# New prices in the planner that orders a two-block layer kernel

## The chip, the cores and the metric

The kernel runs on one core of a Trainium2 chip. The metric is the device time of one execution in microseconds; lower is better. The time before is the median of three executions, 1999.38 us (1998.83 to 1999.78).

## The reference

A sequence of 256 tokens with 1024 features passes through two stacks of two layers, all in float32.

The first stack has two hybrid layers. Each normalises its input, multiplies it by `w_in`, runs a short causal convolution, a gated delta rule in chunks of 64 over four heads, and a second gated convolution; it projects back with `w_out` and adds a gated feed-forward block of width 2816:

```python
def hybrid_layer(x, ...):
    h = rms_norm(x, norm1_g)
    proj = h @ w_in
    ...
    o_dn = chunk_gated_delta_rule(q, k, v, g, beta)
    ...
    x = x + jnp.concatenate([o_dn, o_sc], axis=-1) @ w_out
    h2 = rms_norm(x, norm2_g)
    x = x + (jax.nn.silu(h2 @ ffn_w_gate) * (h2 @ ffn_w_up)) @ ffn_w_down
    return x
```

The second stack has two layers of three sub-blocks each: a feed-forward block, a token mixer, a feed-forward block. Each sub-block's input is normalised and shifted by a modulation vector (`silu(c) @ mod_w`, nine vectors of 1024 per layer), and its output is normalised, scaled and added. The token mixer has a diagonal state-space branch (32 groups of 64 states, a recurrence along the tokens) and an attention branch with a forgetting gate (8 heads), whose results are gated, merged and projected.

## The kernel before, in words

**The products.** Activations lie transposed, features on the 128 partitions and 256 tokens along the row. Every weight matrix is streamed once, in blocks of 128x1024 words (512 KB): eight tiles of 128x128. The products are of type `float32r`; to keep the accuracy, weights and activations are split into a high and a low part, and each tile takes three products (`group`, L258 to L274). `prepare` (L219 to L245) brings one block: a load into `wr` (four buffers) on SP's queue at L228, the high part `wh` by ScalarE (L234; a few by VectorE, L232), the low part `wl` by VectorE (L241; four buffers). `wblk` keeps four blocks (`AHEAD`) prepared ahead of the one in use. A group's sums lie in four PSUM banks with the tag "g", which VectorE or ScalarE must read before the next group may start.

**Work beside the products.** The modulation vectors are 144 steps on VectorE, each with a load of 512 KB into a single buffer `mraw` (`mod_step`, L494 to L502, paced by `MOD_RATE`). `ssm_params` (L1104 to L1192) prepares a layer's state-space tables: it runs inside the feed-forward block ahead of the mixer, as a long chain of 128x512 products on VectorE (L1116, the helper `tt`), then transposes (L1159, copied out by ScalarE at L1160) and small products of 32 columns (L1170). `ssm_tile` (L1194 to L1240) makes the recurrence: products (L1205), VectorE scans (L1218), and small products of 32 columns (L1230, L1237). The delta rule inverts its triangular matrices by rows (L827) and levels (L841 to L856). `narrow` (L295 to L319) makes eight-column projections with 32-column products (L311) on an operand made by VectorE at L303. In `ffn` (L414 to L458) VectorE multiplies the gate and the up group (L445) and with ScalarE splits the result (L372, L373).

**What sets the order.** The program is first written down in its natural order. Then `Order` (L1604 to L1899) takes the list of instructions, makes a graph of them with a price in nanoseconds for each (`price`, L1676 to L1703; loads at L1732 to L1741), latencies between engines (`LAT`) and the releases of buffers, and simulates a list schedule on all engines (`run`). `fix` does so forward and backward in turns, for four settings (`HOW`) of ten rounds each, the priorities of each round coming from the times of the round before, and keeps the plan with the shortest simulated span. The order of the starts in that plan becomes the order of the instructions on each engine. Nothing else of the plan is kept: each engine works through its list in that order, and each instruction still waits for what it needs. A load is two nodes: the issue on its queue, and the transfer at 360 bytes per ns in order of issue, `end`, some latency after the issue; a consumer starts 907 to 1000 ns after the transfer's end (last row of `LAT`):

```python
    LAT = [[0, 196, 197, 224, 240, 0, 0],
           ...
           [907, 1000, 985, 907, 907, 0, 0]]
```

VectorE's price at L1699 is (n + 66)/0.96 ns for an instruction with two full operands of n elements per partition: 1135 ns for n = 1024, 602 ns for n = 512.

Of the kernel before, what the change touches and what calls it, by code (L numbers as in the profile page):

```python
# [1603 lines left out]
class Order:  # L1604
# [71 lines left out]
    def price(s, e, x):  # L1676
        free = lambda y: int(np.prod([n for _, n in list(y.ap)[1:]]))
        real = lambda l: [y for y in l if getattr(y, "bass_ap", None) is not None]
        ins, outs = real(x.ins), real(x.outs)
        psum = any("PSUM" in str(y.bass_ap.space) for y in ins)  # L1680
        n = free(outs[0])
        if e == s.PE:
            n = free(ins[0])
            m = free(ins[1])
            if str(ins[0].dtype).endswith("float32r"):
                return max(n / 2.4, 92 if n > 64 else 80) + 2
            if m <= 32:
                return 150 if n > 64 else 60
            return (1 if getattr(x, "is_transpose", False) else 2) * (max(n / 1.2, 92) + 2)
        n = max(free(y) for y in ins + outs)  # L1690
        ptr = any(free(y) == 1 for y in ins)
        op = str(x.opcode)
        if e == s.DVE:
            if op == "Reciprocal":
                return (6 * n + 66) / 0.96
            if op == "Memset":
                return n / 0.96 + 8
            full = sum(free(y) > 1 or n == 1 for y in ins) > 1 or psum or op == "TensorReduce"
            return ((n if full else n / 2) + 66) / 0.96 + (61 if ptr and op == "TensorScalarPtr" else 0)  # L1699
        if e == s.ACT:  # L1700
            return n / 1.2 + (51 if psum else 94) + (93 if ptr and op == "Activation" else 0)
        same = any(list(y.ap)[-1][0] == 0 for y in ins)
        return 148 + n * (1.667 if same else 2.104)  # L1703


    def trace(s, instructions):
        live, room, rel, slots, alloc, queue = {}, {}, {}, {}, {}, {}
        opened, closed, shut, tags = set(), [], {}, {}
        acc = []
        for x in instructions:  # L1710
            if str(x.opcode) == "TilePoolBoundary":
                acc.append(None)
            else:
                acc.append(s.accesses(x) if len(x.outs) else [])
        last = {}
        for i, a in enumerate(acc):
            for r in a or ():
                last[r[0].name] = i
        for x, a in zip(instructions, acc):
            if a is None:  # L1720
                n = x.bass_pool_name
                if n in opened:
                    opened.discard(n)
                    closed.append(n)
                else:
                    opened.add(n)
                    shut[n] = (s.node(s.NONE, 0), list(closed))
                continue
            if not len(x.outs):
                continue  # L1730
            e = s.NAMES[str(x.engine).split(".")[-1]]
            if str(x.opcode) == "DMACopy":  # L1732
                both = all(getattr(y, "bass_ap", None) is not None and hasattr(y.bass_ap.tensor, "tag_meta") for y in list(x.ins) + list(x.outs))
                i = s.node(e, {s.SP: 650 if both else 475, s.ACT: 100, s.POOL: 1038}[e], x)
                size = max(4 * int(np.prod([n for _, n in y.ap])) for y in list(x.ins) + list(x.outs))
                end = s.node(s.DMA, size / 360.0)
                s.edge(i, end, 650 if e == s.SP else 1100)
                if e in queue:
                    s.edge(queue[e][0], i, 0)
                    s.edge(queue[e][1], end, 0)  # L1740
                queue[e] = i, end  # L1741
            else:
                f = str(getattr(x, "func", "")).split(".")[-1]
                i = end = s.node(e, s.price(e, x), x, s.SETS.get(f) if e == s.ACT else None, s.shares(e, x))
            for r in a:
                t = r[0]
                if t.name in live:
                    continue
                tag = t.tag
                live[t.name] = []  # L1750
                rel[t.name] = s.node(s.NONE, 0)
                if tag in alloc:
                    s.edge(alloc[tag], i, -s.cost[alloc[tag]])
                alloc[tag] = i
                pool = next(n for n in sorted(shut, key=len, reverse=True) if tag.rsplit("_", 1)[0].endswith("_" + n))
                tags.setdefault(pool, []).append(t.name)
                sl = slots.setdefault(tag, [])
                if len(sl) == t.tag_meta.bufs:
                    o = min(sl, key=last.get)
                    sl.remove(o)  # L1760
                    room[t.name] = rel[o]
                else:
                    room[t.name] = shut[pool][0]
                sl.append(t.name)
            for t, w, p0, p1, f0, f1, ps in a:
                hits, keep = 0, []
                for q in live[t.name]:
                    qi, qe, qw, a0, a1, b0, b1 = q
                    hit = a0 < p1 and p0 < a1 and b0 < f1 and f0 < b1
                    hits += hit  # L1770
                    if hit and (w or qw) or ps:
                        near = e == qe and not (hit and qw)
                        s.edge(qi, i, 0 if near else s.LAT[qe][e])
                    if not (ps or w and p0 <= a0 and a1 <= p1 and f0 <= b0 and b1 <= f1):
                        keep.append(q)
                live[t.name] = keep
                if not hits:
                    s.edge(room[t.name], i, s.FREE2[e])
            for t, w, p0, p1, f0, f1, ps in a:
                live[t.name].append((end, s.eng[end], w, p0, p1, f0, f1))  # L1780
                s.edge(end, rel[t.name], s.FREE1[s.eng[end]])
        for n, (i, before) in shut.items():
            for o in before:
                for t in tags.get(o, ()):
                    s.edge(rel[t], i, 0)
# [137 lines left out]
```

## Time and profile before

| | |
|---|---|
| Median of three executions | 1999.38 us |
| The profiled execution's own time | 2000.42 us |
| Its span, first to last instruction | 1998.3 us |
| TensorE (PE) busy | 1888.2 us, 94% |
| VectorE (DVE) busy | 1516.6 us, 76% |
| ScalarE (ACT) busy | 1075.8 us, 54% |
| Read from memory | 380.12 MB, 191 GB/s |
| Chain that ended last, by engine | PE 84%, DVE 8%, ACT 3%, DMA 3%, issue 2% |
| Mean granted TensorE clock | 0.970 |

The share of an engine is its busy time over the span. The chain that ended last is followed back from the last instruction; each piece is an instruction or a transfer that the next piece waited for.

### The profile page before, as it was taken

The numbers are of one execution on the slowest core, as the hardware profiler recorded it, in microseconds if no ns is written. First come the engines' busy times: TensorE is split into PE (matmuls) and PEld (weight loads), VectorE is DVE, ScalarE is ACT, GpSimd is POOL, SyncE is SP. The second block draws the span as 40 slices with busy tenths as digits, with TensorE's granted clock in tenths as the row PEclk, the third lists the DMA queues.
The fourth block names the chain that finished last, engine by engine and source line by source line (L and its number), as shares of the span: only waits on it lengthen the run. The fifth ranks groups of instructions, "written<-read, shape, count | busy, mean of one in ns | idle before, by whom it ended". The sixth has DMA issues, their size and how long they took to land.

```text
span 1998.3 us, 40034 instructions
## 1 busy us (share of the span) xinstructions
PE 1888.2 (94%) x16106; PEld 1830.1 (92%) x16106; DVE 1516.6 (76%) x2826; ACT 1075.8 (54%) x1976; POOL 8.4 (0%) x20
## 2 busy tenths in 40 slices
PE   6999999899899986999999986999999999999998
PEld 6999999899899986999889986998999889999997
DVE  7888977898877788976784798867876677477554
ACT  6766544675544464445555653445554556565443
POOL 0000000000000000000000000000000000000000
PEclk8999999899999998999899998999999999999999
DMA  5334778433577763775343644775687443344553
GB/s 191 126 116 154 281 274 294 158 138 113 201 275 274 278 213 132 264 267 201 100 150 128 214 160 142 263 260 190 221 292 261 166 138 128 138 169 148 180 190 116
DMA packets 110921, 384.82 MB, mean 193 GB/s; under 512 B 16400, under 2 KB 16912, under 8 KB 110736
## 3 DMA queue, kind: packets, MB, share of 16 engines
q1 hardware_dynamic: 110448, 381.88, 54.5%
q8 instruction: 126, 2.06, 0.4%
q14 instruction: 59, 0.48, 0.1%
q10 hardware_dynamic: 288, 0.39, 0.1%
HBM read 380.12 MB, written 1.05 MB: 191 GB/s over the span
## 4 chain that ended last, share of the span: by engine, by line
PE 84%; DVE 8%; ACT 3%; DMA 3%; issue 2%; SPq 0%; DVEq 0%; ACTq 0%
PE g L271 72%; PE g L291 3%; DVE wl L241 2%; DMA mraw<-in_modw 1%; DMA wr<-in_wstream 1%; DVE smi L1116 1%; DVE stb L1116 1%; PE m L1205 1%; DVE scp L1116 1%; ACT wh L234 1%; PE m L853 1%; PE m L848 1%; DVE xs L135 1%; PE m L1159 0%; PE m L1293 0%
## 5 line engine op out<-in xcount | busy, mean ns | idle before, releaser
L271 PE MATMUL g<-xh,wh 128*128 128x256 f32 (+1 forms) x3264 | 918.1, 288 | 26.0 <-ACT xh L389 8.5
L271 PE MATMUL g<-xl,wh 128*128 128x256 f32 x3264 | 922.4, 286 | 7.9 <-DVE xl L390 7.9
L271 PE MATMUL g<-xh,wl 128*128 128x256 f32 (+1 forms) x3264 | 911.3, 286 | 2.8 <-DVE wl L241 2.8
L241 DVE TENSOR_TENSOR wl<-wr,wh 128x1024 fp32r<-128x1024 f32 (+1 forms) x576 | 697.0, 1214 | 253.4 <-PE g L271 134.4
L234 ACT CAST wh<-wr 128x1024 fp32r<-128x1024 f32 (+1 forms) x528 | 551.2, 1047 | 513.5 <-PE g L271 271.8
L271 PEld LDWEIGHTS g<-xh,wh 128*128 128x128 f32 x3264 | 617.5, 192 | 35.5 <-ACT xh L389 10.9
L271 PEld LDWEIGHTS g<-xl,wh 128*128 128x128 f32 x3264 | 626.1, 192 | 10.2 <-DVE xl L390 8.9
L271 PEld LDWEIGHTS g<-xh,wl 128*128 128x128 f32 x3264 | 618.7, 192 | 4.7 <-DVE wl L241 3.6
L271 PE MATMUL g<-ah,wl 128*128 128x256 f32 x880 | 246.1, 280 | 0.0
L271 PE MATMUL g<-ah,wh 128*128 128x256 f32 x880 | 246.0, 280 | 0.0
L271 PE MATMUL g<-al,wh 128*128 128x256 f32 x880 | 245.7, 279 | 0.0
L501 DVE SCALAR_TENSOR_TENSOR mraw<-mraw,siluc 128x1024 f32<-128x1024 f32 x144 | 175.8, 1221 | 32.0 <-DMA mraw<-in_modw 31.4
L271 PEld LDWEIGHTS g<-al,wh 128*128 128x128 f32 x880 | 165.8, 188 | 0.0
L271 PEld LDWEIGHTS g<-ah,wh 128*128 128x128 f32 x880 | 164.8, 187 | 0.3 <-issue 0.2
L271 PEld LDWEIGHTS g<-ah,wl 128*128 128x128 f32 x880 | 165.0, 188 | 0.0
L372 ACT CAST ah<-act 128x256 fp32r<-128x256 f32 x132 | 49.4, 404 | 60.8 <-DVE act L445 60.7
L445 DVE TENSOR_TENSOR act<-g,sg 128x256 f32<-128x256 f32 x132 | 52.1, 420 | 16.7 <-PE g L271 14.2
L373 DVE TENSOR_TENSOR al<-act,ah 128x256 fp32r<-128x256 f32 x132 | 52.3, 420 | 12.0 <-ACT ah L372 10.2
L432 ACT ACTIVATE sg<-g 128x256 f32<-128x256 f32 x108 | 40.3, 384 | 36.6 <-PE g L271 36.4
L1159 PE MATMUL m<-cst,stb 128*128 128x128 f32 x64 | 12.9, 364 | 28.5 <-DVE stb L1116 28.5
L1159 PEld LDWEIGHTS m<-cst,stb 128*128 128x128 f32 x64 | 10.8, 192 | 29.5 <-DVE stb L1116 29.5
L271 PE MATMUL g<-gl,wh 128*128 128x256 f32 x128 | 36.0, 281 | 0.0
(454 smaller groups left out, 2135.7 us busy)
## 6 DMA issues: line engine op xcount, KB each, us to landing
wr<-in_wstream SPq DMA_DIRECT2D x568, 512.0 KB, 4.3
mraw<-in_modw SPq DMA_DIRECT2D x144, 512.0 KB, 4.2
wr<-in_wstream SPq DMA_DIRECT2D x8, 256.0 KB, 5.0
stb<-in_ssmc SPq DMA_DIRECT2D x2, 512.0 KB, 3.2
sbb<-in_ssmb SPq DMA_DIRECT2D x2, 512.0 KB, 4.0
up<-u SPq DMA_DIRECT2D x32, 32.0 KB, 1.9
x<-in_x SPq DMA_DIRECT2D x2, 256.0 KB, 5.3
x<-in_x SPq DMA_DIRECT2D x1, 512.0 KB, 7.2
```

Of the source, the lines that this page charges most:

```text
L135: nc.vector.scalar_tensor_tensor(out=a, in0=s.z[:, k, :], scalar=s.gains[:, k:k + 1], in1=s.rho, op0=ALU.mult, op1=ALU.mult)
L234: nc.scalar.copy(out=hi[:, :n], in_=raw[:, :n])
L241: e.tensor_tensor(out=lo[:, :n], in0=raw[:, :n], in1=hi[:, :n], op=ALU.subtract)
L271: nc.tensor.matmul(ps[c][:, :x.shape[-1]], wt, x, start=(bi == 0 and k == 0 and i == 0), stop=(bi == len(specs) - 1 and k == n - 1 and i = ...
L291: nc.tensor.matmul(ps[h], x(k0 + k)[:, h * P:(h + 1) * P], wt[:, k, :], start=(k0 == 0 and k == 0 and i == 0), stop=(k0 + k == kt - 1 and ...
L372: s.nc.scalar.copy(out=out_h, in_=src)
L373: s.nc.vector.tensor_tensor(out=out_l, in0=src, in1=out_h, op=ALU.subtract)
L432: nc.scalar.activation(out=a, in_=gp[c][:, :T], func=AF.Silu)
L445: nc.vector.tensor_tensor(out=a, in0=up[c][:, :T], in1=sg[c], op=ALU.mult)
L501: nc.vector.scalar_tensor_tensor(out=w, in0=w, scalar=1.0, in1=s.sc_, op0=ALU.mult, op1=ALU.mult, accum_out=s.mod[l][:, j:j + 1])
L1116: tt = lambda o, a, b, op: V.tensor_tensor(out=o, in0=a, in1=b, op=op)
L1159: PE.transpose(tp[:, n * P:(n + 1) * P], a[:, j + n // 2, n % 2].rearrange("p t r -> p (t r)"), s.ident)
```

## The change

Only `Order`'s prices change, so only the order of the instructions on each engine (and on the DMA queues) can differ.

- A `float32r` product of n columns was max(n/2.4, 92) + 2 ns and is max(0.4453 n + 4.5, 94) (for n over 64): 108.7 ns becomes 118.5 ns at 256 columns, 215.3 becomes 232.5 at 512.
- A float32 product with at most 32 columns of weights was 150 ns (n over 64) or 60 ns and is 110 or 45.
- Another float32 product was twice (once for a transpose) max(n/1.2, 92) + 2 and is twice (once) max(0.844 n, 109): 217.3 becomes 218 at 128 columns, 188 becomes 218 at 64 or fewer.
- A scan on VectorE was (n + 66)/0.96 ns and is (2n + 47)/0.96: 135 becomes 182 at n = 64.
- A load issued on SP was 475 ns of the queue and is 374 (a copy within the chip's SBUF stays at 650). The latency between issue and transfer was 650 ns on SP and is 1500; on other queues it was 1100 and is 1950.

```diff
@@ price
             if str(ins[0].dtype).endswith("float32r"):
-                return max(n / 2.4, 92 if n > 64 else 80) + 2
+                return max(0.4453 * n + 4.5, 94 if n > 64 else 82)
             if m <= 32:
-                return 150 if n > 64 else 60
-            return (1 if getattr(x, "is_transpose", False) else 2) * (max(n / 1.2, 92) + 2)
+                return 110 if n > 64 else 45
+            return max(0.844 * n, 109) * (1 if getattr(x, "is_transpose", False) else 2)
...
             if op == "Memset":
                 return n / 0.96 + 8
+            if getattr(x, "is_tensor_tensor_scan", False):
+                return (2 * n + 47) / 0.96
@@ trace
-                i = s.node(e, {s.SP: 650 if both else 475, s.ACT: 100, s.POOL: 1038}[e], x)
+                i = s.node(e, {s.SP: 650 if both else 374, s.ACT: 100, s.POOL: 1038}[e], x)
                 size = max(4 * int(np.prod([n for _, n in y.ap])) for y in list(x.ins) + list(x.outs))
                 end = s.node(s.DMA, size / 360.0)
-                s.edge(i, end, 650 if e == s.SP else 1100)
+                s.edge(i, end, 1500 if e == s.SP else 1950)
```

## Rows read from the trace of the kernel before

**Rows 1.** The page, parts 1 and 2: busy time, and granted clock in 40 slices

```profile
PE 1888.2 (94%) x16106; PEld 1830.1 (92%) x16106; DVE 1516.6 (76%) x2826; ACT 1075.8 (54%) x1976; POOL 8.4 (0%) x20
...
PEclk8999999899999998999899998999999999999999
```

**Rows 2.** Waits of PE, whole span: us in total, times, longest

```profile
PE m L1159 <- DVE stb L1116: 28.5, 4, 12.7
PE g L311 <- DVE sqb L303: 13.4, 1, 13.4
PE g L271 <- ACT xh L389: 8.5, 7, 3.3
PE g L271 <- DVE xl L390: 7.9, 4, 3.4
...
PE g L271 <- DVE wl L241: 2.8, 4, 1.3
...
PE m L853 <- ACT Y L850: 0.3, 1, 0.3
```

**Rows 3.** Busy time by stretch: PE, PEld, DVE, ACT, POOL, clock, DMA

```profile
250.00:300.00 50.00, 50.00 (x424) 50.00 (x423) 39.25 (x56) 22.85 (x34) 0.00 (x0) 1.00 0.78 275
50.00:170.00 120.00, 117.39 (x992) 115.45 (x990) 103.41 (x254) 77.80 (x223) 0.00 (x0) 1.00 0.36 127
990.00:1140.00 150.00, 150.00 (x1480) 139.90 (x1479) 104.67 (x202) 84.87 (x165) 0.00 (x0) 1.00 0.47 163
741.00:782.00 41.00, 26.00 (x213) 25.20 (x211) 40.44 (x64) 10.44 (x16) 0.00 (x0) 0.86 0.35 129
1181.00:1222.00 41.00, 25.55 (x209) 24.75 (x207) 40.14 (x63) 10.45 (x16) 0.00 (x0) 0.87 0.34 128
767.00:790.00 23.00, 8.74 (x77) 8.11 (x79) 18.52 (x31) 5.08 (x10) 3.03 (x5) 0.63 0.15 53
```

**Rows 4.** Timeline of DVE, 764 to 783 us: start us, us, instruction

```profile
764.03 1.22 DVE L241 TENSOR_TENSOR wl<-wr,wh 128x1024 fp32r<-128x1024 f32 x1
765.16 0.69 DVE L1116 TENSOR_TENSOR smi<-scp,ssm_lam 128x512 f32<-128x512 f32 x1
765.77 0.68 DVE L1116 TENSOR_TENSOR scp<-scp,ssm_lam 128x512 f32<-128x512 f32 x1
...
781.47 0.69 DVE L1116 TENSOR_TENSOR stb<-stb,smi 128x512 f32<-128x512 f32 x1
...
782.60 0.42 DVE L445 TENSOR_TENSOR act<-g,sg 128x256 f32<-128x256 f32 x1
782.94 1.21 DVE L241 TENSOR_TENSOR wl<-wr,wh 128x1024 fp32r<-128x1024 f32 x1
```

**Rows 5.** Timeline of PE at the end of that stretch

```profile
780.16 0.48 PE L1159 MATMUL m<-cst,stb 128*128 128x128 f32 x1 [12.68 <-DVE stb L1116]
```

**Rows 6.** The page, part 6: loads, KB each, median us from issue to landing

```profile
wr<-in_wstream SPq DMA_DIRECT2D x568, 512.0 KB, 4.3
mraw<-in_modw SPq DMA_DIRECT2D x144, 512.0 KB, 4.2
...
up<-u SPq DMA_DIRECT2D x32, 32.0 KB, 1.9
```

**Rows 7.** Waits of DVE and of SP's queue for the modulation loads, whole span

```profile
DVE mraw L501 <- DMA mraw<-in_modw: 31.4, 36, 3.3
...
SPq L500 <- DVE mraw L501: 267.5, 79, 10.2
```

**Rows 8.** Chain that ended last, around 703 to 711 us: start us, us, what

```profile
703.30 5.23 DMA mraw<-in_modw
...
709.86 1.14 DVE wl L241
711.00 0.34 DVE x L476
```

**Rows 9.** Timeline of PE just behind it

```profile
711.47 0.36 PE L271 MATMUL g<-xh,wh 128*128 128x258 f32 x1 [1.97 <-DVE x L476]
```

**Rows 10.** Timeline of PE: narrow and 32-column products, start us, us

```profile
34.59 1.93 PE L311 MATMUL g<-x,sqb 128*32 128x256 f32 x16 [13.36 <-DVE sqb L303]
...
997.13 1.09 PE L1237 MATMUL yp<-pa,scp 128*32 128x63 f32 x64
```

**Rows 11.** Timeline of DVE: a run of scans

```profile
987.28 0.65 DVE L1218 TENSOR_TENSOR_SCAN st<-ssm_r,pa 128x64 f32<-128x64 f32 x3
```

## The prediction

> **What bounds the kernel now.** I read the page first: PE is busy 1888 of 1998 us and no other engine comes near [rows 1]. So PE's idle time, about 110 us, with the dips of the granted clock beside it [rows 1], is all that an order can give back; and it can spoil more. Next the stretches: in a feed-forward stretch PE makes 424 products in 50 us without a gap, 117.9 ns each, and the whole of the second mixer's middle, 150 us, has no idle at all; the first mixer's 120 us lose 2.6 [rows 3]. The idle time lies elsewhere, and the list of PE's waits names it: 28.5 us before the transposes of the state-space tables, 13.4 once at the start, and some 3 us at a time where a sub-block begins and waits for its split input [rows 2]. Third, the timeline inside the largest wait, which comes once per layer of the second stack. From 765 to 782 VectorE does nothing but table products; the product that frees the PSUM banks (the multiplication at L445) and the next low weights stand behind them [rows 4], and PE, whose four prepared blocks are used up, waits 12.7 us [rows 5]. In the 41 us of the chain PE is idle for 15.0 in the one layer and 15.4 in the other, and from 767 to 790 us the granted clock averages 0.63, so part of what follows ran at 1.2 rather than 2.4 GHz [rows 3].
>
> **What is right and wrong in the old prices.** One float32r product costs the plan 108.7 ns before and 118.5 after; the trace has 117.9 [rows 3]. VectorE was priced right already: 1135 ns for low weights, against 1.13 from one start to the next, and 602 for a table product, against 0.61 [rows 4]. So the old plan ran PE 8% too fast beside a right VectorE; the new one keeps them in step. This price is the change's main part: 424 products by 9.8 ns are 4.2 us of plan in every 50.
>
> The Trainium skill, page "TensorE: Matmul & The Clock Gate", section "Wait — 56ns, not 53.3ns?", gives the start-to-start time of warm products as N/2.4 GHz plus about 2.5 ns: 109.2 ns at 256 columns. That speaks against this change: by it the old price is right and the new plan has PE 8% too slow. By 117.9 the forecast below stands; by 109.2 its gains fall away and the second rival would be the likeliest, near 2007. The measured 424 in 50 us decide against the rule here, so it gets no chance of its own.
>
> Loads. From issue to a consumer's start the old plan counts 0.475 + 0.65 + 1.456 + about 0.99 = 3.57 us for 512 KB and the new one 0.374 + 1.5 + 1.456 + 0.99 = 4.32; the trace has 4.3 and 4.2 [rows 6]. Two parts go the other way. A copy of `u` within SBUF lands after 1.9 us [rows 6] and becomes 0.65 + 1.5 + 0.09 + 0.9 = 3.1 in the plan. And the narrow projection's products at L311: a float32 product is two instructions, so 16 instructions in 1.9 us are eight products of 240 ns [rows 10], priced 150 before and 110 after. The small ones at L1237, 32 products (64 instructions) in about 0.9 us, 28 ns each [rows 10], come nearer: 60 becomes 45. Scans: three in 0.65 us, the last of which is 0.27 long, so 0.19 apart [rows 11]; 135 becomes 182. The other float32 prices move by under 1 ns at 128 columns, and 30 at 64 or fewer. All these are short beside a group of products, and I put them at nothing: they lie under PE's products in stretches without idle [rows 3]. If that cover were gone, the `u` copies would cost their 1.2 us twice, and the eight narrow products, called 40 ns too cheap each beyond the old price, 0.3 us four times.
>
> **The sum, part by part.** The work is the same, so each term is a wait that shrinks or grows.
>
> First, the two table stretches. One more block of weights ahead of the chain gives PE 24 products, 2.83 us, and costs VectorE 1.13. The ends: nothing, if the order stays, and 15 us each if it is spread out [rows 3]; on the other side one wait more of the longest kind, +13.4 [rows 2]. What moves is small: 213 products by 9.8 ns, 2.1 us more PE work in each stretch of the plan [rows 3]. Against a plan that let PE wait 12.7 us, that is nearer to the lower end. I take those 2.1 us twice: −4.2.
>
> Second, the modulation loads. VectorE stood 36 times before a step whose load hadn't landed, 31.4 us, 0.87 each [rows 7]; the plan's landing moves by 0.75, so most of these go. On PE they cost little: at 703 us the load is on the chain that ended last, low weights and the last addition follow it [rows 8], and PE loses 1.97 us [rows 9]. The ends are 0 and −27 (36 by 0.75); I take the one visible place, −2.0. SP's queue is the risk here: 79 times the next modulation load waited for its buffer, 267.5 us in all, up to 10.2 at once, with the weight loads queued behind it [rows 7]. If such a load moves ahead of a weight load, the weights come late; but PE has waited for low weights 2.8 us in all [rows 2], four blocks being ready, so 0, with +10.2 as the end for one bad place.
>
> Third, the margin. With PE priced too fast, a small product stood in PE's list where the plan had its operand just ready; on the chip PE came there 8% later and found it ready. The levels' update waited for its operand once, 0.3 us [rows 2]. The first mixers have 48 products of levels, 16 turns and 30 rows, 94 hand-overs in 240 us, 2.6 us apart; 8% of that is 0.21 us. With 48 hand-overs of the attention, 142 by 0.21 = 30 us is the end if every one used up its margin; 0 the other. VectorE's prices fit, so most operands will be ready: I take a twentieth, +1.5.
>
> The start: 13.4 us before L311 [rows 2], whose operand VectorE makes late in its list. No price there asks for another place: 0, with −13.4 as the bound.
>
> Sum: −4.2 − 2.0 + 1.5 = −4.7 on the profiled execution's 2000.42, which is 1.04 above the median of the runs shown: 1995.7, and 1994.7 as a median.
>
> **Rivals.** *The table stretches dissolve.* With PE seen as the fuller engine, the plan puts L445 and four or five blocks of weights between the table products: 4.5 blocks by 2.83 fill 12.7 us. For it: VectorE has room behind it, as its busy share in the feed-forward stretch is 39 of 50 [rows 3]. Against: both layers lose the same 15 us [rows 3], so it is no accident of one place, and the tables' products keep their place in PE's full list. 1999.4 − 30 − 2 + 1.5 = 1969.
>
> *Just in time.* The margin above is used up by a third: +10, less the 2.0 of the loads, 2007.4. Its place are levels, rows and attention; for it, 150 us of the second mixer without one wait show that today's order is safe, and an order cannot better that; against it, the right prices of VectorE. It decides once these waits pass about 10 us, 0.07 per hand-over.
>
> *The change does nothing that counts.* Where PE never waits, a new order of the same work costs the same; if the waits at sub-block starts and tables stay as they are, 1999.4.
>
> **How the numbers follow.** A measurement of this kernel tells about 0.2%, 4 us, from no change. Forecast 0.31 (its own range 1988 to 1996), tables dissolved 0.10, nothing that counts 0.29, just in time 0.30. Faster by more than 4 us is the first two, 0.41; same 0.29; slower 0.30. The time is the likeliest case's, 1994.7. The range reaches from 1974, which leaves out most of the dissolved tables, to 2010, which leaves out the upper part of just in time and the one bad place of the loads on top of it.
>
> **What would show it.** Right: PE's wait for the table transposes falls from 28.5 to about 24; VectorE's wait for modulation loads falls from 31.4 to under 10; the 424 products in 50 us stay. Just in time would show as new PE waits for ScalarE's or VectorE's results at the levels (L848, L853), the rows (L827) and the attention, above 10 us together. Dissolved tables would show low weights between the table products and no PE wait above 3 us there. The forecast is wrong if PE's idle time appears in the mixers' middle, if table stretches grow, or if PE waits for weights because a modulation load holds SP's queue.

## The result, and the profile after

The change makes the kernel faster by 1.1%: a median of 1974.48 us in four executions (1972.97 to 1983.94) against 1999.56 for the kernel before on the same chip (1998.83 to 1999.78), a ratio of 0.9891 with a 95% interval of 0.9865 to 0.9916. The forecast was 1994.7 with a range of 1974 to 2010. Its sign was right and its size was a fifth of what came. The time lies half a microsecond inside the lower end of the range, and, as will be seen, more than half of the gain came from places for which the forecast had no gain.

The profiled execution took 1974.74 us with a span of 1972.9, against 2000.42 and 1998.3. First the page of the kernel after, busy time and granted clock, which answers to [rows 1]:

```profile
PE 1880.0 (95%) x16106; PEld 1825.2 (93%) x16106; DVE 1514.3 (77%) x2826; ACT 1074.0 (54%) x1975; POOL 8.3 (0%) x20
...
PEclk8999999999999998999999998999999999999999
```

The work is the same: 16106 instructions on PE and 2826 on VectorE in both. PE's idle time (span less busy) falls from 110.1 to 92.9 us, 17.2 less. Its busy time falls by 8.2, and with it goes a mean granted clock of 0.976 instead of 0.970: fewer products run at 1.2 GHz behind a wait. Next PE's waits after, which answer to [rows 2]; columns as there:

```profile
PE m L1159 <- DVE stb L1116: 28.5, 4, 12.7
PE g L311 <- issue: 9.6, 1, 9.6
PE g L271 <- ACT xh L141: 7.9, 2, 5.1
PE g L271 <- DVE xl L390: 7.3, 2, 3.7
PE g L271 <- ACT xh L389: 6.3, 7, 1.9
PE g L311 <- DVE xs L1339: 4.2, 2, 2.2
PE g L271 <- DVE wl L241: 2.6, 4, 1.1
...
PE g L311 <- DVE xc L702: 1.2, 1, 1.2
```

The largest wait, for the table transposes, has not moved by a tenth. The wait at the start, 13.4 before, is 9.6. ("issue" means that the profile shows nothing that the engine waited for.) What else shrinks are many small waits at the beginnings and ends of sub-blocks. L311 waits 1.2 us for `xc` now; before it was:

```profile
PE g L311 <- DVE xc L702: 3.9, 1, 3.9
```

The stretches of [rows 3], moved to where the same work now stands (the feed-forward one in place, then what the prediction calls the second mixer's middle, which is the middle of the first token mixer of the second stack, and the two table stretches):

```profile
250.00:300.00 50.00, 50.00 (x424) 50.00 (x422) 40.20 (x58) 24.39 (x35) 0.00 (x0) 1.00 0.79 285
...
971.00:1121.00 150.00, 150.00 (x1485) 140.75 (x1484) 103.99 (x204) 84.20 (x165) 0.00 (x0) 1.00 0.47 163
723.80:764.80 41.00, 26.15 (x214) 25.34 (x212) 40.48 (x65) 10.53 (x16) 0.00 (x0) 0.88 0.35 129
1162.30:1203.30 41.00, 25.84 (x211) 25.07 (x209) 40.36 (x63) 10.65 (x16) 0.00 (x0) 0.86 0.35 128
```

424 products in 50 us, no idle in the mixer's middle, 14.9 and 15.2 us idle at the tables: where PE was full it stays full, and where it stood longest it still stands. VectorE's wait for the modulation loads, [rows 7], went the other way from what the prediction said:

```profile
DVE mraw L501 <- DMA mraw<-in_modw: 44.3, 52, 2.8
```

So where are the 25 us? Since PE runs the same 16106 instructions in a similar sequence, the two traces can be laid side by side by their count (a float32 product counts twice; at the borders of a part the lists differ by some products). The table is worked out from the starts of PE's instructions in the profiled execution of each kernel: the time that each part of the count took before, and the difference from that in the kernels of this study (their labels are explained below).

```
products             before  after    e1    e2    e3    e4    e7   e11
0-200 (start)          44.6   -4.2  -1.8  -3.8  -4.4   0.0  -4.6  -4.5
200-1400 (mixer 1)    145.4   +1.0  -0.9  +8.3  +9.7  -1.0  +1.5  +0.3
FFN, first stack      319.8   +0.8 +11.3  +0.7  +0.7   0.0  +1.7  +0.6
three transitions     104.7  -14.2 -12.0  +2.2  +6.3  -2.6 -10.6 -10.8
rest of mixer 2        82.9   +1.2  +2.3  +0.9  +0.5  -0.4  +1.1  +2.3
5500-7600 (tables)    268.0   -4.0  -0.4  +0.7  +1.2  +4.0  -7.3  -2.9
9300-11600 (tables)   292.6   -1.1  -3.0  -3.9  -3.0  -0.9  -3.3  -6.6
14700-15000           46.4    -3.4  -3.6  -2.4  -3.9  -1.2  -5.3  -3.6
all other parts       686.8   -1.8  +1.8  +2.9   0.0  -0.7  -0.6  +1.1
whole                1991.3  -25.7  -6.3  +5.6  +7.1  -2.9 -27.5 -24.0
```

Mixer 1 and mixer 2 are those of the first and second hybrid layer. The feed-forward row is products 1400 to 2800 and 4200 to 5500. The three transitions are the start of the second hybrid layer's mixer (2800 to 3000), the end of its delta rule (3600 to 3900) and the start of its feed-forward block (4000 to 4200). They hold more than half of the gain, 14.2 us. Here they are as stretches of the kernel before, in the columns of [rows 3]:

```profile
357.10:389.40 32.30, 25.59 (x203) 24.16 (x202) 29.53 (x67) 19.08 (x36) 0.62 (x1) 0.84 0.38 129
460.30:501.00 40.70, 38.19 (x303) 36.66 (x302) 31.91 (x78) 22.57 (x86) 0.00 (x0) 0.96 0.33 117
513.00:544.80 31.80, 26.64 (x203) 25.61 (x202) 28.27 (x54) 19.68 (x36) 0.00 (x0) 0.95 0.49 175
```

And the same products in the kernel after:

```profile
353.90:380.70 26.80, 24.46 (x202) 23.71 (x201) 26.14 (x61) 17.71 (x33) 0.31 (x1) 0.94 0.37 120
453.10:489.00 35.90, 35.76 (x301) 34.87 (x301) 30.35 (x73) 23.10 (x86) 0.00 (x0) 1.00 0.38 133
500.80:528.60 27.80, 25.42 (x203) 24.33 (x202) 27.58 (x53) 19.12 (x35) 0.00 (x0) 1.00 0.60 200
```

Of the first, 4.4 us of the gain are idle time (6.71 becomes 2.34) and 1.1 busy time at a better clock (0.84 becomes 0.94); of the second 2.4 and 2.4; of the third 2.8 and 1.2. In these places small products with long chains behind them (normalisation, the delta rule's last turns) alternate with group products. In the list after, the two products of the normalisation at L354 in the third transition stand 7 and 11 places earlier among PE's products, and the first of L923 and L927 in the second stand 23 earlier. It is tempting to read from this that an earlier place makes the chain ready in time, but that is not shown: e2 and e3 have the two of L354 7 and 17 places earlier, and PE is idle for 6.1 us in the third transition there, against 5.2 before and 2.4 after.

### The profile page after: what moved, and what is told of

The parts are those of the page before. It is cut to its first block, busy times and chain, and to the rows that moved or that the text cites. A ratio compares the mean times of both kernels' runs of the same rounds, so it can differ in the third digit from the quotient of the medians.

```text
span 1972.9 us, 40030 instructions
## 1 busy us (share of the span) xinstructions
PE 1880.0 (95%) x16106; PEld 1825.2 (93%) x16106; DVE 1514.3 (77%) x2826; ACT 1074.0 (54%) x1975; POOL 8.3 (0%) x20
## 4 chain that ended last, share of the span: by engine, by line
PE 78%; DVE 11%; ACT 5%; DMA 4%; issue 2%; SPq 0%; DVEq 0%; ACTq 0%
PE g L271 66%; DMA mraw<-in_modw 3%; PE g L291 3%; DVE wl L241 2%; DVE smi L1116 1%; DVE scp L1116 1%; ACT wh L234 1%; DVE stb L1116 1%; DVE mraw L501 1%; PE m L1205 1%; DVE xs L135 1%; PE m L1159 1%; PE m L1170 1%; PE m L848 1%; PE m L853 1%
## 5 line engine op out<-in xcount | busy, mean ns | idle before, releaser
L271 PE MATMUL g<-xh,wh 128*128 128x256 f32 (+1 forms) x3264 | 919.0, 287 | 22.3 <-ACT xh L141 7.9
L271 PE MATMUL g<-xl,wh 128*128 128x256 f32 x3264 | 925.2, 286 | 7.3 <-DVE xl L390 7.3
L271 PE MATMUL g<-xh,wl 128*128 128x256 f32 (+1 forms) x3264 | 913.8, 286 | 2.6 <-DVE wl L241 2.6
L271 PEld LDWEIGHTS g<-xh,wh 128*128 128x128 f32 x3264 | 617.2, 191 | 30.5 <-ACT xh L141 9.7
L271 PEld LDWEIGHTS g<-xl,wh 128*128 128x128 f32 x3264 | 624.7, 192 | 9.0 <-DVE xl L390 7.9
L271 PEld LDWEIGHTS g<-xh,wl 128*128 128x128 f32 x3264 | 618.7, 192 | 5.1 <-DVE wl L241 3.4
L271 PE MATMUL g<-ah,wl 128*128 128x256 f32 x880 | 246.0, 280 | 0.0
L271 PE MATMUL g<-ah,wh 128*128 128x256 f32 x880 | 245.4, 279 | 0.1
L271 PE MATMUL g<-al,wh 128*128 128x256 f32 x880 | 245.4, 279 | 0.0
L501 DVE SCALAR_TENSOR_TENSOR mraw<-mraw,siluc 128x1024 f32<-128x1024 f32 x144 | 175.8, 1221 | 44.8 <-DMA mraw<-in_modw 44.3
L271 PEld LDWEIGHTS g<-al,wh 128*128 128x128 f32 x880 | 165.5, 188 | 0.0
L271 PEld LDWEIGHTS g<-ah,wl 128*128 128x128 f32 x880 | 165.0, 188 | 0.0
L271 PEld LDWEIGHTS g<-ah,wh 128*128 128x128 f32 x880 | 164.5, 187 | 0.4 <-issue 0.3
L445 DVE TENSOR_TENSOR act<-g,sg 128x256 f32<-128x256 f32 x132 | 53.5, 420 | 12.6 <-PE g L271 7.7
L432 ACT ACTIVATE sg<-g 128x256 f32<-128x256 f32 x108 | 39.8, 384 | 38.0 <-PE g L271 38.0
L1159 PE MATMUL m<-cst,stb 128*128 128x128 f32 x64 | 13.1, 373 | 28.5 <-DVE stb L1116 28.5
L1159 PEld LDWEIGHTS m<-cst,stb 128*128 128x128 f32 x64 | 11.2, 197 | 29.5 <-DVE stb L1116 29.5
L271 PE MATMUL g<-gl,wh 128*128 128x256 f32 x128 | 36.0, 281 | 0.0
```

The lines of the kernel that those rows point to most:

```text
L271: nc.tensor.matmul(ps[c][:, :x.shape[-1]], wt, x, start=(bi == 0 and k == 0 and i == 0), stop=(bi == len(specs) - 1 and k == n - 1 and i = ...
L432: nc.scalar.activation(out=a, in_=gp[c][:, :T], func=AF.Silu)
L445: nc.vector.tensor_tensor(out=a, in0=up[c][:, :T], in1=sg[c], op=ALU.mult)
L501: nc.vector.scalar_tensor_tensor(out=w, in0=w, scalar=1.0, in1=s.sc_, op0=ALU.mult, op1=ALU.mult, accum_out=s.mod[l][:, j:j + 1])
L1159: PE.transpose(tp[:, n * P:(n + 1) * P], a[:, j + n // 2, n % 2].rearrange("p t r -> p (t r)"), s.ident)
```

## The experiments

Two readings of the result stood against each other, beside the prediction's own. **In step**: the plan's engines must agree about time, and the prices of float32r products and of loads are the two that keep PE, VectorE and the queue in step. **A new draw**: any change of a price makes the planner settle on another plan, and some plans happen to be better. In the expectations theory R is the new draw and theory P the two prices in step; theories F and L, held ahead of e1 to e4, say that the float32r price alone or the landing of loads alone is the change. All twelve kernels compute the whole reference, and all differ from one of the two kernels in the planner alone. Ratios are to the kernel before on the same chip, whose median was between 1998.37 and 2000.24.

### One price at a time: e1, e2, e3, e4

e1, the float32r price alone:

```diff
-                return max(n / 2.4, 92 if n > 64 else 80) + 2
+                return max(0.4453 * n + 4.5, 94 if n > 64 else 82)
```

> Only the float32r price is new (108.7 to 118.5 ns at 256 columns); small products, scans and loads keep the old prices. Theory F (the float32r price is the change: the old plan put small products behind too many float32r products, so what hangs on them on VectorE came late): 1970 to 1980 us, nearly all of the 25 us. Theory L (the landing of loads is the change): 1995 to 2003. Theory R (any change of prices draws another order, the gain is luck of the draw): anywhere from 1975 to 2010, and without a pattern over the four runs.

Measured: 1994.05 us, ratio 0.9976 (0.9962 to 0.9989).

e2, the loads alone:

```diff
-                i = s.node(e, {s.SP: 650 if both else 475, ...
+                i = s.node(e, {s.SP: 650 if both else 374, ...
-                s.edge(i, end, 650 if e == s.SP else 1100)
+                s.edge(i, end, 1500 if e == s.SP else 1950)
```

> Only issue and landing of loads are new. Theory F: 1995 to 2003 us, as before. Theory L: 1970 to 1980, and VectorE's wait for modulation loads under 31 us. Theory R: anywhere from 1975 to 2010.

Measured: 2009.02 us, ratio 1.0052 (1.0034 to 1.0071). Slower.

e3, the kernel after with the old float32r price put back:

```diff
-                return max(0.4453 * n + 4.5, 94 if n > 64 else 82)
+                return max(n / 2.4, 92 if n > 64 else 80) + 2
```

> All new prices but that of float32r products. Theory F: 1995 to 2003 us. Theory L: 1970 to 1980. Theory R: anywhere, and not the sum of the runs with single prices.

Measured: 2007.88 us, ratio 1.0048 (1.0030 to 1.0066). Slower too.

e4, the other products and the scans alone (the price of products of 32 columns, of the other float32 products, and the two new lines for scans; float32r and loads as before):

```diff
-                return 150 if n > 64 else 60
-            return (1 if getattr(x, "is_transpose", False) else 2) * (max(n / 1.2, 92) + 2)
+                return 110 if n > 64 else 45
+            return max(0.844 * n, 109) * (1 if getattr(x, "is_transpose", False) else 2)
...
+            if getattr(x, "is_tensor_tensor_scan", False):
+                return (2 * n + 47) / 0.96
```

> Only the prices of the other products and of the scans are new. Theories F and L: 1995 to 2003 us, as before. Theory R: as far from before as the other runs, 10 us or more to either side.

Measured: 1993.79 us, ratio 0.9982 (0.9967 to 0.9996).

What follows: no part alone gives the gain. Theories F and L both fail: F wanted 1970 to 1980 in e1, L in e2 and e3, and e2 and e3 are slower than either theory allowed. Theory R did no better in e4, for which it wanted 10 us or more to either side. On top of the kernel before the float32r price is worth 5 us; on top of the rest of the change it is worth 33 (2007.88 to 1974.48). The loads alone cost 10. A sum of terms, as the prediction made it, can't hold this: the parts don't add. It also shows that VectorE's wait for modulation loads is no measure of the time: it is 22.0 us in e2 and 18.9 in e3, both slower than before (31.4), and 44.3 in the faster kernel after.

### The pair: e7, e11

e7, the float32r price and the loads, no small products and no scans:

```diff
-                return max(n / 2.4, 92 if n > 64 else 80) + 2
+                return max(0.4453 * n + 4.5, 94 if n > 64 else 82)
...
-                i = s.node(e, {s.SP: 650 if both else 475, ...
+                i = s.node(e, {s.SP: 650 if both else 374, ...
-                s.edge(i, end, 650 if e == s.SP else 1100)
+                s.edge(i, end, 1500 if e == s.SP else 1950)
```

> The float32r price and the loads' prices are new, small products and scans old. Theory P (the two prices work as a pair: the float32r price sets the small products and VectorE's chains right, and with it the loads must not be taken for landed too early): 1972 to 1982 us, no loss in the feed-forward stretches where the float32r price alone lost 5.6 and 5.7 us, and in the first mixers the gains of the float32r price. Theory R (luck of the draw): between 1985 and 2010, losses at places of no pattern.

Measured: 1974.04 us, ratio 0.9883 (0.9865 to 0.9901).

e11, as e7, with the issue on SP left at 475:

```diff
-                return max(n / 2.4, 92 if n > 64 else 80) + 2
+                return max(0.4453 * n + 4.5, 94 if n > 64 else 82)
...
-                s.edge(i, end, 650 if e == s.SP else 1100)
+                s.edge(i, end, 1500 if e == s.SP else 1950)
```

> The float32r price and the later landing are new, the issue on SP keeps 475 ns. If the landing is the loads' half of the pair: 1970 to 1980 us. If the issue is: 1988 to 1998, as with the float32r price alone.

Measured: 1976.30 us, ratio 0.9882 (0.9861 to 0.9904).

The float32r price and the landing of loads are the whole change; the issue price, the small products and the scans add nothing on top that these runs can tell. The table by products shows which price does what, place by place:

- *The start* (−3.5 to −4.8) comes with every plan that has the new landing: after, e2, e3, e7, e11, and e5 and x1 below. Without it, it is −1.8 (e1) and 0.0 (e4).
- *The three transitions* (−10.4 to −14.2) gain in every plan that has the new float32r price, e5 and x1 below among them; with the loads alone or all but it they lose 2.2 and 6.3, and e4 gains 2.6.
- *The feed-forward blocks of the first stack* lose 11.3 us in e1, where the float32r price is new and the landing old; in after, e7 and e11 that loss is at most 1.7.
- *The mixer of the first hybrid layer* loses 8.3 and 9.7 us in e2 and e3, where the landing is new and the float32r price old; with both it is at most 1.5.

Each price brings a gain, and each alone brings a loss that the other takes away. What the loss in e1 looks like can be read at 230 to 243 us, in the first of the two feed-forward blocks, which is work without one gap before. Parts of the timelines of e1, first ScalarE, then VectorE, then PE (start us, us, instruction, in brackets the wait and what ended it), and last the stretch behind the wait in the columns of [rows 3]:

```profile
230.75 1.05 ACT L234 CAST wh<-wr 128x1024 fp32r<-128x1024 f32 x1 [3.59 <-DMA wr<-in_wstream]
233.89 1.05 ACT L234 CAST wh<-wr 128x1024 fp32r<-128x1024 f32 x1 [2.09 <-DMA wr<-in_wstream]
...
234.98 1.23 DVE L241 TENSOR_TENSOR wl<-wr,wh 128x1024 fp32r<-128x1024 f32 x1 [1.92 <-ACT wh L234]
237.50 1.23 DVE L501 SCALAR_TENSOR_TENSOR mraw<-mraw,siluc 128x1024 f32<-128x1024 f32 x1 [1.30 <-DMA mraw<-in_modw]
238.65 0.08 DVE L501 DVE_READ_ACCUMULATOR mraw<-mraw,siluc 128x1 f32 x1
238.65 0.75 DVE L445 TENSOR_TENSOR act<-g,sg 128x256 f32<-128x256 f32 x2
...
235.95 0.29 PE L271 MATMUL g<-xh,wl 128*128 128x256 f32 x1
239.22 0.43 PE L271 MATMUL g<-xh,wh 128*128 128x256 f32 x1 [2.98 <-DVE act L445]
239.45 0.42 PE L271 MATMUL g<-xl,wh 128*128 128x256 f32 x1
...
239.20:243.00 3.80, 3.78 (x19) 3.80 (x20) 3.45 (x7) 3.15 (x6) 0.00 (x0) 0.55 0.81 276
```

ScalarE waits 3.59 and 2.09 us for weights here, but waits of that size stand in this block before and in e11 too (3.8 and 4.6 at most) and cost PE 0.3 us there at most. What is different is VectorE's list: it has a modulation step whose load hasn't landed, presumably because the old landing price called it landed. VectorE stands 1.30 us for it, and the multiplication at L445, which frees PE's banks, is queued behind that wait and the step's own 1.15 us. PE waits 2.98. The next products then start 0.22 us apart instead of 0.118: from 239.2 to 243.0 the granted clock averages 0.55, that is, most of the stretch at 1.2 GHz rather than 2.4, and 19 products take 3.8 us, 1.6 more than at full clock. The place costs PE 4.6 of the 5.6 us that this block loses, 1.30 of them the late load itself. (The second block loses 5.7; its longest wait, 1.6 us, is for ScalarE's `sg` at L432.) In e11, with the new landing, VectorE waits for modulation loads about as often in the same stretch of 190 to 360 us (7.8 us, 10 times; 8.4 and 11 in e1), but PE waits 0.3 us there in all: a wait with nothing behind it that PE needs is free.

### Is it a lucky draw? e5, e6

e5 is the kernel after, e6 the kernel before, each with 1 ns added to a float32r product (in e5 to those of more than 64 columns), which hardly changes the balance between the engines but lets the planner choose anew:

```diff
-                return max(0.4453 * n + 4.5, 94 if n > 64 else 82)
+                return max(0.4453 * n + 5.5, 95 if n > 64 else 82)
```

```diff
-                return max(n / 2.4, 92 if n > 64 else 80) + 2
+                return max(n / 2.4, 92 if n > 64 else 80) + 3
```

> The changed kernel with 1 ns more for each float32r product, a price no less true to the trace than its own. Theory P: within 5 us of the changed kernel, 1970 to 1980. Theory R: 10 us or more away.

> The kernel before with 1 ns more for each float32r product, 109.7 for 108.7. Theory P: within 5 us of before, 1994 to 2004, perhaps a tenth of the way to the changed kernel. Theory R: 10 us or more away on either side.

Measured: e5 1977.78 us, ratio 0.9896 (0.9877 to 0.9914); e6 1993.65, ratio 0.9980 (0.9968 to 0.9991). The gain survives in the one and doesn't arise in the other, so it is not the luck of one draw: four plans with the pair (after, e5, e7, e11) lie between 1974 and 1978, three without either price (before, e4, e6) between 1993 and 2000. But a new draw is worth something: e6 gained 0.2% by it. That is as much as e1 and e4 gained, so neither of those two can be told from a redraw. The draw shows within the gain as well. If the time from each product's start to the next is put down to the line of the later one, the kernel after gains 9.8 us at L311 (29.7 to 19.9) and 7.8 at L271 (1637.5 to 1629.7); e7, just as fast, gains 3.2 and 18.7. The sum is a matter of prices, the place of each microsecond is not. No run sets both prices well above the measured times, so whether they must be right or only higher than the old ones is not shown.

### The wait that stayed: x1, e8

The table stretches are the largest wait of both kernels. If right prices don't dissolve it, is it VectorE's capacity or the order? x1 is the kernel after with one thing more: in each round of the planner the table chain on VectorE (whatever writes `smi`, `scp` or `stb`) gets a priority as if 40 us later, so that the low weights and L445 go first. e8 is the same on the kernel before.

```diff
+        late = [i for i in range(n) if s.eng[i] == s.DVE and s.ins[i] is not None
+                and s.ins[i].outs[0].bass_ap.tensor.name.split("_")[0] in ("smi", "scp", "stb")]
         best = None
         for how in HOW:
...
                 prio = [MIXP * b - (1 - MIXP) * a for a, b in zip(back, end)]
+                for i in late:
+                    prio[i] += 40000
```

> The changed kernel, with the priority of VectorE's table products put 40 us later in every round of the planner after the first. If the two waits of 12.7 us before the table transposes are only a matter of the order (VectorE has room behind them): 1943 to 1953 us, PE's wait at L1159 under 5 us. If VectorE's work is what bounds these stretches: 1970 to 1980, the waits moved to other lines.

> The kernel before, old prices, with the table products' priority put 40 us later as in the run before. If the table waits have nothing to do with the prices: about 37 us under before, 1958 to 1966. If the new prices are needed for it: less than half of that, 1980 to 1999.

Measured: x1 1937.59 us, ratio 0.9697 (0.9678 to 0.9716); e8 1949.74, ratio 0.9752 (0.9722 to 0.9782). x1 beats both kernels: 37 us faster than the kernel after; e8 is 50 us faster than the kernel before. Both are below what was expected of the order alone (1943 to 1953, and 1958 to 1966). The timeline of VectorE in x1, inside what was a solid run of table products in [rows 4]:

```profile
744.33 0.68 DVE L1116 TENSOR_TENSOR smi<-scp,ssm_lam 128x512 f32<-128x512 f32 x1
744.94 2.35 DVE L241 TENSOR_TENSOR wl<-wr,wh 128x1024 fp32r<-128x1024 f32 x2
747.21 0.68 DVE L1116 TENSOR_TENSOR scp<-scp,smi 128x512 f32<-128x512 f32 x1
747.82 1.21 DVE L241 TENSOR_TENSOR wl<-wr,wh 128x1024 fp32r<-128x1024 f32 x1
```

And the page of x1, busy time:

```profile
PE 1874.3 (97%) x16106; PEld 1818.1 (94%) x16106; DVE 1507.1 (78%) x2826; ACT 1069.2 (55%) x1973; POOL 8.2 (0%) x20
```

Low weights stand between the table products, and PE no longer waits at L1159. By products, 5500 to 7600 and 9300 to 11600 gain 22.4 and 20.6 us against the kernel before, where the change gains 4.0 and 1.1. So it was the order, and no price of this change touches it. Between x1 and e8 0.55% is left, some 11 us, for the new prices: less than the 25 they give by themselves. By products, e8 gains 4.9 us in the transitions and 2.8 at 14700 to 15000 without them, so a part of the places is mended by both.

### Small products moved by hand: e9, e10

By the prediction's third term a plan with PE too fast puts small products behind their operands with a margin; the traces suggest that it puts them too late for those who need the result. To tell these apart, e9 takes the kernel before and lists every small product up to 1 us earlier; e10 takes the kernel after and lists each up to 1 us later. PE's list alone changes. The edit's bound (`floor`) is weaker than the expectation says: it follows an operand back to PE's own earlier products and counts no time for the work of ScalarE and VectorE between. So a product can stand ahead of the moment at which the plan has its operand ready. e10 has the sign turned and its bound, taken from the successors, likewise counts PE alone. The step of e9 that moves the products, behind the lines that make `floor`:

```diff
...
+        for i in range(n):
+            if s.eng[i] == s.PE and s.ins[i] is not None:
+                g = s.ins[i].outs[0].bass_ap.tensor.name.split("_")[0] == "g"
+                if g == False:
+                    key[i] = max(key[i] - shift, min(key[i], floor[i] + 1.0))
```

> The kernel before with only PE's list changed: products that don't belong to a group of weights stand up to 1 us (eight float32r products) earlier, no earlier than what they wait for in the plan. Lateness theory (the cheap float32r price put small products behind too many others, and VectorE's chains waited for them): 1984 to 1993 us, gains where a normalisation or the delta rule's chain ends. Margin theory (that place was a safety margin): slower than before, 2002 to 2012, with new waits of PE at the small products.

> The changed kernel with only PE's list changed: the same products up to 1 us later, no later than the first of PE's own instructions that needs them. Lateness theory: slower than the changed kernel by 5 to 15 us, 1979 to 1990. Margin theory: as fast or faster, 1968 to 1976, with fewer waits of PE.

Measured: e9 2104.58 us, ratio 1.0520 (1.0501 to 1.0539); e10 2092.51, ratio 1.0454 (1.0431 to 1.0478). Both expectations missed by far: either move costs over 100 us on its base. The experiment changed more than it meant to. The longest groups of PE's waits in e9 that the kernel before lacks (L853 has 0.3 us there):

```profile
...
PE m L853 <- ACT Y L850: 10.9, 24, 0.5
...
PE m L1287 <- ACT aW L1283: 7.0, 11, 0.9
...
PE m L810 <- DVE UT L854: 5.8, 15, 0.4
PE m L1293 <- ACT pT L1289: 5.7, 11, 0.7
```

In the kernel before, the levels of several heads go through PE in batches: an instruction of L853 starts 0.124 us after the one before it (11.9 us for 96). Moved one by one, each against its own bound, the batches break: the 96 stand in 31 runs before and in 48 in e9. PE often comes to a hand-over before the operand is ready, and from the instruction before it to one of L853 there are 0.298 us in e9 and 0.274 in e10. PE's switches between group and small products rise from 502 to 722, and from 546 to 762. Waits like those at L853 are what the prediction's rival "just in time" looked for. They don't occur in the kernel after, where L853 waits for nothing that the profile lists. Whether lateness or margin acted at a given transition, these two runs can't settle. In the third transition they lean to lateness: e10 puts the two products of L354 back by 7 and 8 places, and the part takes 2.7 us longer than in the kernel after; e9 puts them 9 places earlier, and PE's idle time there falls from 5.2 to 4.1. But other small products moved with them, and e2 and e3 speak against the place of L354 as the cause.

## Why the prediction was right in sign and wrong in size

That the time fell into the range is luck: 1974.48 against a lower end of 1974, which was set to leave out most of the dissolved tables, and outside the forecast's own 1988 to 1996. The sign is luck in part, since it came from the terms for the tables and the loads, and neither came as told. Of the three signs that were to show the forecast right, one came, the 424 products in 50 us.

**Where PE is full, nothing changes: right.** 424 products in 50 us and the mixer's middle are as before. By the rule of the Trainium skill, page "TensorE: Matmul & The Clock Gate", section "Wait — 56ns, not 53.3ns?", a product of 256 columns would take an estimated 109.2 ns, and the old price would be right. The trace after disagrees with it as the trace before did: 424 `float32r` products in 50 us are 117.9 ns each. With the old price back in the rest of the change (e3) the kernel is 33 us slower; that shows what the price is worth to the order, not how long a product takes.

**First term, the tables, −4.2: the real wait didn't move.** It is 28.5 us, four times, 12.7 at most, in both traces. The step that failed is that more PE work in the plan moves a block of low weights ahead of the chain; why 2.1 us per stretch did not do it, no run shows. The 4.0 and 1.1 us that the two parts gain lie elsewhere, in part at L1170, which comes after the chain and whose wait falls from 3.0 to 0.6. The rival that dissolves the table wait did not occur either; x1 and e8 show that another priority does it, and what it is worth: 37 us after the change and 50 before, where the rival had 30.

**Second term, the loads, −2.0: the reasoning fell.** VectorE's waits for `mraw` were to go below 10 us and rose to 44.3. The step that failed is "the plan's landing moves by 0.75, so most of these go". The same line in e1, e2 and e7:

```profile
DVE mraw L501 <- DMA mraw<-in_modw: 61.7, 60, 2.8
...
DVE mraw L501 <- DMA mraw<-in_modw: 22.0, 28, 2.0
...
DVE mraw L501 <- DMA mraw<-in_modw: 45.5, 60, 1.8
```

With the loads' prices it is lower, 22.0 for 31.4 alone and 45.5 for 61.7 beside the float32r price, but by less than a third, and a mere redraw moves it as much (45.3 in e6). With the float32r price, which the term left out, it is higher by more than that (61.7 in e1). The one PE wait the term was priced from did shrink (L476, 2.0 us before, now 0.6 in two), but in e6 it shrinks as much. The landing price's worth is another one, and larger: without it the float32r price loses 11 us in the feed-forward blocks (e1), and with it the start gains 4.

**Third term, the margin, +1.5: no loss came, and the waits behind the gain had no term. This is the step that mis-sized the forecast.** The prediction saw the 8% by which PE ran too fast in the plan only as a safety margin that the right price would use up. In the three transitions the kernels that have it beside the landing gained 10.4 to 14.2 us (after, e5, e7, e11), and e1 12.0. No sign of a lost margin is there: the levels' waits went from 0.3 to nothing, the rows' from 1.1 (twice) to 1.2. The prediction had the 3-us waits at sub-block starts before it [rows 2] and gave them no term and no reason for that. That the float32r price acts at the transitions is shown by the runs with and without it. How it does so stays open: in the kernel after, small products stand earlier there, but e2 and e3 have L354 as early and wait longer, and e9 failed to isolate it.

**The start, 0 with −13.4 as the bound: too cautious.** L303 moves up in VectorE's list (from 34.31 to 20.09 us), and L311 starts at 31.09 instead of 34.59, and no longer waits for VectorE:

```profile
31.09 1.94 PE L311 MATMUL g<-x,sqb 128*32 128x256 f32 x16 [9.64 <-issue]
```

The statement "no price there asks for another place" failed: the landing price does, in every plan that has it.

**The other prices, nothing: right on top of the pair** (e7 is as fast as the kernel after), and alone no more than a redraw (e4).

**Rivals.** "Just in time" (2007) and "nothing that counts" did not occur. What had no place among the terms was the interaction. Each price was costed by itself against the old plan, and the two that matter, loads and float32r, are worth +10 and −5 alone and −24 together. The small forecast rested on the sum.

## What to carry to other kernels

Prices in a planner can act together, as these two did, so mend those of all engines that meet, at once; one right price among wrong ones can make the order worse (e2, e3), and then the pair must be tried before the price is thrown away. Look for the gain of better prices where sub-blocks meet, not in full stretches nor in the longest wait. A long wait that two plans with different prices share to the tenth of a microsecond may be a matter of priority; here it was, and telling the planner so was worth more than the prices (x1, e8). Redraw a plan with a price changed by a nanosecond before believing a gain of two thousandths.

## What the runs showed that was not expected

- Right order is worth more than full engines suggest: x1 leaves all work as it is, and PE goes from 94% to 97% busy with 14 us less busy time, at a mean granted clock of 0.988 instead of 0.970: waits also cost clock behind them. After PE's wait of 2.98 us in e1 the granted clock averages 0.55 for the next 3.8 us.
- A float32r product that follows a float32 one takes longer to come in: in the kernel before 0.20 us lie between the first and the second product behind a run of L1205 (988.21 to 988.41, 989.83 to 990.03), where 0.12 is usual. Over the 209 places of that kernel where PE goes from small to group products without a wait, the median is 0.20 too; the other way, from a group product to a small one, it is 0.12, so as a rule nothing is lost there. Of the 220 switches more in e9, 110 are of the dear kind, which at 0.08 us would be some 9 of its 105 us. PE's idle time there grows by 56 us (110.1 to 166.5), and its busy time by 47 in all. The timeline of PE in the kernel before at the first of the two places:

```profile
988.21 0.37 PE L271 MATMUL g<-xh,wh 128*128 128x256 f32 x1
988.41 0.28 PE L271 MATMUL g<-xl,wh 128*128 128x256 f32 x1
988.53 0.28 PE L271 MATMUL g<-xh,wh 128*128 128x256 f32 x1
```
